# Second score pass on 128 rows for the dilated and grouped-query heads, with each key's two parts on both row halves

## The chip, the cores and the metric

The kernel runs on one core of one Trainium2 chip. The metric is device time in microseconds (us) of one launch; lower is better. A core has a matrix engine (TensorE, PE in the rows; its weight loads are PEld), a vector engine (VectorE, DVE), a scalar engine (ScalarE, ACT), a general engine (GpSimd, POOL) and an engine that issues the DMA transfers of this kernel (SyncE, SP). Each engine takes its own instructions in a fixed order.

## What is computed

The reference is an encoder of two layers on 512 tokens of width 1024. Each layer runs three groups of attention heads on the same input, projects their joined outputs and normalises, then runs a gated feed-forward block and normalises again. The part that the change touches is the first product of two of the three groups, in which every query meets every key:

```python
for l in range(DEPTH):                       # 2 layers
    h = x @ w_in[l]
    ...
    out_a = dense_attention(qa, ka, va, (64 + 32) ** -0.5)      # 6 latent heads, query and key of 96
    out_b = dilated_mixture(qb, kb, vb, rel_bias)               # 6 heads of 64, bias and mask per distance
    out_c = dense_attention(qc, kc, vc, 64 ** -0.5)             # 4 query heads on 2 key heads, of 64
    mix = concatenate([out_a, out_b, out_c]) @ w_out[l]
    x = layer_norm(ALPHA * x + mix)
    x = layer_norm(ALPHA * x + (silu(x @ w_gate[l]) * (x @ w_up[l])) @ w_down[l])
```

All data are 32-bit floats. The kernel keeps this accuracy by writing a number as a rounded first part plus a small second part and by multiplying the parts in separate passes, which add up in the same accumulator.

## The kernel before

The 512 tokens are four tiles of 128 rows. In each layer the work goes: value projection of the dilated heads, query and key projection of the first pair of dilated heads (`dil_qk(0)`), the attention proper (`attend`), the output projection, a normalisation, and the feed-forward block in two parts.

`attend` walks over 64 units, a unit being one head and one tile of 128 queries: six dilated heads, then four grouped-query heads, then six latent heads, four units each. For a unit, `Head.a` multiplies the query tile with all 512 keys into a bank `sc` (line 241), VectorE takes the minimum (line 247 for the dilated heads, which adds the bias tile `dt`; line 251 for the others), ScalarE the exponential (253), VectorE the reciprocal of the sum (255), and GpSimd the product into `pl` (256). One unit later `Head.b` transposes `pl` on TensorE into a bank `ptr` (264), and ScalarE and VectorE write its two parts `PTh` and `PTl` (271, 272). Another unit later `Head.c` multiplies with the values into `po` (282, 283). `sc` and `ptr` have two banks each, so a bank comes free only when VectorE has read it.

Between the units stand fillers: the projections of the next pairs (`dil_qk(1)`, `dil_qk(2)`, in the rows `qkp`), of the grouped-query heads (`g2`, rows `tp`), of the latent heads (`g1`, rows `tp`; `uq`, `uv`, `kT`), and part of the output projection (`opp`). A table `W` says at which units they begin and end. The tile framework's own scheduler then fixes the order of every engine's instructions from this program; so an edit at one place can move instructions elsewhere.

A head of 64 elements has a product of three passes: query first part with key first part, query second part with key first part, query first part with key second part. The query of a dilated or grouped-query head is stored with its two parts on the two halves of the 128 rows (`qa[:, e]`, first part on rows `64*e` and up). The key's first part lies on both halves, so one pass of all 128 rows does the first two products. The third is a second pass on the 64 rows of the query's first part:

```python
r, kc = cb(lst())
return [(qa[:, e, c], ka[:, kb]), (qa[r, e, c], kc)]
```

For a dilated pair the key comes from `dil_qk`: `dk` (a `pmix` slot) holds the two parts of both heads' keys, each head on its 64 rows, and `dqk` (a `pqk` slot) receives each head's first part on both halves by four copies on SyncE's queue (line 565). For the grouped-query heads both parts already lie on both halves (`gkk` holds each key head twice). The latent heads have queries and keys of 96 rows and three passes of 96 rows (`qk_of`).

One more place is spoken of below: the gains `gg` of the grouped-query heads are loaded at the start of each layer's program (line 410) into a single slot and scaled on VectorE (line 411). The scheduler puts the second layer's load and scaling into the first layer's attention, just behind the last use of the first layer's gains (line 430).

Of the kernel before, what the change touches and what calls it, by code (L numbers as in the profile page):

```python
# [10 lines left out]
F32 = mybir.dt.float32  # L11
# [5 lines left out]
P = 128  # L17
# [64 lines left out]
def encoder(ctx: ExitStack, tc, x, w_in, mla_q_norm, mla_kv_norm, w_uq, w_ukv, gqa_q_norm, gqa_k_norm, rel_bias,  # L82
# [59 lines left out]
    def wload(src, shape, lo, ring="w", raw="w"):  # L142
        # a weight chunk in two parts whose sum is exact
# [51 lines left out]
    def layer_norm(t, gb, end=False):  # L195
# [6 lines left out]
        if end:  # L202
            # nothing follows: the shortest way from the statistics to the result
# [16 lines left out]
    def load_gb(g, b):  # L220
        # the one-element copy holds the loads back until the slots are wanted
# [9 lines left out]
    class Head:  # L231
# [4 lines left out]
        def a(self, qt):  # L236
            # logits (negated), their minimum, exponentials over their sum
# [21 lines left out]
        def b(self, qt):  # L259
            # keys on partitions, in two parts  # L260
# [33 lines left out]
    class Pair:  # L294
        # the two heads of one 128-row tile of the mix
# [16 lines left out]
    def attend(heads, fillers):  # L312
        # the last pair goes by halves of the queries, so that the first half is done earlier
# [28 lines left out]
    def token_proj(xT, l, c0, c1, evac, lo, order=PAIRS, ws=None, pools=None):  # L342
        # order: (token tile, weight chunk) steps
# [24 lines left out]
    def bias_tables():  # L368
        # relative bias plus branch count, negated, as one vector over key - query
# [12 lines left out]
        # one copy a query, each a word further on, so that a row step of 1024 words shifts by one query  # L382
# [14 lines left out]
    for l in range(DEPTH):  # L397
        mix = [None] * 8

        # grouped-query heads: queries, keys, values with tokens on partitions  # L400
# [5 lines left out]
        # gains of the grouped-query heads, the query's with minus the logit scale  # L406
# [8 lines left out]
        def evac_g2(t, pb):  # L415
# [26 lines left out]
            # each query head in two parts side by side, each key head twice  # L442
# [10 lines left out]
        # dilated heads: values  # L453
# [7 lines left out]
        # latent projections  # L461
# [42 lines left out]
        def to_T(src, n, dst):  # L504
            # [tokens, n] tiles to [n, tokens] in two parts
# [35 lines left out]
        def dil_qk(pair):  # L541
            ws = [wload(krows(w_in[l], 0, KD, c + pair * P, c + pair * P + P), (P, KD, P), LO['qk'], QKR[pair]) for c in (C_Q, C_K)]
            yield
            for q, (h, o) in zip((True, False), ws):
# [5 lines left out]
                # per head: the query's two parts, the key's first part twice, on all partitions  # L550
                r = pqk.tile([P, 2, T], F32R, tag="q", name="dqk")
                if q:
                    sc = -(HD ** -0.5)
# [5 lines left out]
                else:  # L559
                    m = pmix.tile([P, 2, T], F32R, tag="m", name="dk")  # L560
                    A.copy(m[:, 0], pb)
                    V.tensor_tensor(m[:, 1], pb, m[:, 0].bitcast(F32), op=ALU.subtract)
                    for e in range(2):
                        for b in range(2):
                            nc.sync.dma_start(r[64 * b:64 * b + 64, e].bitcast(F32), m[64 * e:64 * e + 64, 0].bitcast(F32))
                    dqk[pair] += [r, m]
                yield

        def rope32(v, nh, tm):
            # v [P, NT, nh, 32], rotated in place  # L570
# [35 lines left out]
        def out_part():  # L606
            # the output projection of the pairs that are done, onto the residual
# [32 lines left out]
        def qk2_of(lst, e, kb, cb):  # L640
            # two passes: the query's two parts against the key's first, its first against the key's second
            def qk(qt):
                qa, ka = lst()[:2]
                c = slice(qt * P, (qt + 1) * P)
                r, kc = cb(lst())
                return [(qa[:, e, c], ka[:, kb]), (qa[r, e, c], kc)]
            return qk

        def qk_of(lst, e, n=64):
            # the three passes of one query tile; the stored order is (key, query) or (query, key) as told  # L650
# [8 lines left out]
        # told: what has been put into the program, for the asserts on the order of its parts  # L659
# [3 lines left out]
        for h in range(6):  # L663
            if h % 2 == 0:
                pr = Pair(mix, 3 + h // 2)
            heads.append(Head(qk2_of(lambda p=h // 2: dqk[p], h % 2, h % 2,
# [90 lines left out]
        for t in (2, 3):  # L757
            out_rest(t, (0, 1, 2))
            finish(t)
        xT = xT2[0]  # L760

        # feed-forward
        f0 = 0
        for part, nf in enumerate((12, 10)):
            act = []
# [96 lines left out]
```

## Time and profile before

| | |
|---|---|
| time, median of 3 runs | 1304.83 us (1304.62 to 1306.63) |
| span of the profiled execution, first to last instruction | 1300.4 us |
| outside the span, against the median | 4.4 us |
| TensorE busy | 1273.2 us, 98% |
| weight loads busy | 1057.4 us, 81% |
| VectorE busy | 678.0 us, 52% |
| ScalarE busy | 539.7 us, 42% |
| GpSimd busy | 323.4 us, 25% |
| first to last score of layer 1, of layer 2 | 60.6 to 269.6 us, 697.8 to 903.8 us |

How to read it: TensorE's busy time is a union of intervals whose ends are modelled, and one matmul's interval reaches into the next one's. So a busy TensorE may still be held up; what a matmul really takes is read from the distance between the starts of two matmuls that follow each other. The other engines' busy shares are means over stages of very different load.

### The profile page before, as it was taken

The page shows a single profiled execution, that of the slowest core. Times are in us where ns is not written, and L with a number is a line of the kernel's source. Part 1 is how long each engine was busy: PE and PEld are TensorE (multiplying, and loading weights), DVE is VectorE, ACT ScalarE, POOL GpSimd, SP SyncE. Part 2 cuts the span into 40 slices and gives each one's busy share as a digit, 9 for nine tenths or more (in the row PEclk, how much of TensorE's full clock was granted, in tenths as well). Part 3 has the DMA queues.
Part 4 walks back from the last instruction along what each step waited for, and adds up shares of the span by engine and source line. Part 5 has one row for each costly group of instructions (what it writes and reads, how often), then busy time and mean ns, then how long its engine had stood idle before and what let it go on. Part 6 is the DMA issues. An engine that isn't in the chain of part 4 may idle for free.

```text
span 1300.4 us, 16747 instructions
## 1 busy us (share of the span) xinstructions
PE 1273.2 (98%) x6352; PEld 1057.4 (81%) x6352; DVE 678.0 (52%) x1132; ACT 539.7 (42%) x949; POOL 323.4 (25%) x344
## 2 busy tenths in 40 slices
PE   8799899999999999999999999999999999999997
PEld 7678778879888888888897787888888888888885
DVE  4248788586333233333663778876933333333345
ACT  3256687554222212222244657866432221222222
POOL 0145465463000000000154455645700000000004
PEclk9899999999999999999999999999999999999999
DMA  6742310233333333332435222104343323333322
GB/s 189 205 120 76 96 33 18 89 99 97 101 96 97 97 97 97 98 98 97 148 87 148 59 88 70 38 13 130 87 118 97 96 93 94 101 96 96 97 101 109
DMA packets 142376, 125.72 MB, mean 97 GB/s; under 512 B 7212, under 2 KB 114860, under 8 KB 142296
## 3 DMA queue, kind: packets, MB, share of 16 engines
q1 hardware_dynamic: 142296, 124.66, 32.0%
q8 instruction: 50, 0.82, 0.3%
q14 instruction: 30, 0.25, 0.1%
HBM read 117.80 MB, written 5.27 MB: 95 GB/s over the span
## 4 chain that ended last, share of the span: by engine, by line
PE 89%; DMA 4%; DVE 4%; POOL 1%; ACT 1%; issue 0%; SPq 0%; DVEq 0%; POOLq 0%; ACTq 0%
PE up L167 6%; PE gate L167 6%; PE gate L165 6%; PE up L165 6%; PE gate L166 6%; PE up L166 6%; PE down L167 6%; PE sc L241 6%; PE down L165 6%; PE down L166 6%; PE ptr L264 4%; PE tp L166 2%; PE tp L167 2%; PE tp L165 2%; PE po L283 2%; PE po L282 2%
## 5 line engine op out<-in xcount | busy, mean ns | idle before, releaser
L152 ACT CAST whi<-wraw 128x1024 fp32r<-128x1024 f32 (+3 forms) x202 | 205.6, 1019 | 555.2 <-PE gate L166 146.3
L156 DVE TENSOR_TENSOR wlo<-wraw,whi 128x1024 fp32r<-128x1024 f32 (+3 forms) x170 | 208.3, 1227 | 319.6 <-ACT whi L152 315.4
L256 POOL TENSOR_TENSOR pl<-pl,srec 128x512 f32<-128x512 f32 x128 | 135.4, 1059 | 159.9 <-DVE srec L255 144.4
L191 POOL TENSOR_TENSOR rstd<-mv,eps_l 128x1 f32<-128x1 f32 x16 | 5.7, 358 | 680.6 <-DVE mv L200 680.6
L166 PE MATMUL gate<-xTl,whi 128*128 128x512 f32 (+1 forms) x384 | 142.8, 372 | 0.0
L166 PE MATMUL up<-xTl,whi 128*128 128x512 f32 (+1 forms) x384 | 142.7, 372 | 0.0
L167 PE MATMUL gate<-xTh,wlo 128*128 128x512 f32 (+1 forms) x384 | 142.7, 372 | 0.0
L167 PE MATMUL up<-xTh,wlo 128*128 128x512 f32 (+1 forms) x384 | 142.7, 372 | 0.0
L165 PE MATMUL up<-xTh,whi 128*128 128x512 f32 (+1 forms) x384 | 142.6, 372 | 0.0
L165 PE MATMUL gate<-xTh,whi 128*128 128x512 f32 (+1 forms) x384 | 142.4, 371 | 0.0
L167 PE MATMUL down<-whi,act 128*128 128x512 f32 x352 | 136.7, 389 | 0.0
L165 PE MATMUL down<-whi,act 128*128 128x512 f32 x352 | 136.7, 389 | 0.0
L166 PE MATMUL down<-wlo,act 128*128 128x512 f32 x352 | 136.7, 389 | 0.0
L156 POOL TENSOR_TENSOR wlo<-wraw,whi 128x512 fp32r<-128x512 f32 (+2 forms) x64 | 79.2, 1259 | 92.9 <-ACT whi L152 91.4
L776 DVE TENSOR_TENSOR sg<-sg,up 128x512 f32<-128x512 f32 x44 | 30.3, 688 | 135.8 <-PE up L167 134.4
L271 ACT CAST PTh<-ptr 128x512 fp32r<-128x512 f32 x128 | 74.9, 585 | 48.1 <-PE ptr L264 47.2
L272 DVE TENSOR_TENSOR PTl<-ptr,PTh 128x512 fp32r<-128x512 f32 x128 | 87.3, 683 | 13.5 <-ACT PTh L271 12.9
L166 PEld LDWEIGHTS up<-xTl,whi 128*128 128x128 f32 x384 | 72.3, 188 | 12.6
L167 PEld LDWEIGHTS up<-xTh,wlo 128*128 128x128 f32 x384 | 72.3, 188 | 12.4
L167 PEld LDWEIGHTS gate<-xTh,wlo 128*128 128x128 f32 x384 | 72.3, 188 | 12.5
L166 PEld LDWEIGHTS gate<-xTl,whi 128*128 128x128 f32 x384 | 72.3, 188 | 12.5
L165 PEld LDWEIGHTS gate<-xTh,whi 128*128 128x128 f32 x384 | 72.3, 188 | 12.4
(176 smaller groups left out, 2499.2 us busy)
## 6 DMA issues: line engine op xcount, KB each, us to landing
wraw<-in_ffn_w_down SPq DMA_DIRECT2D x54, 512.0 KB, 3.6
wraw<-in_ffn_w_up SPq DMA_DIRECT2D x44, 512.0 KB, 3.8
wraw<-in_ffn_w_gate SPq DMA_DIRECT2D x44, 512.0 KB, 3.8
wraw<-in_w_in SPq DMA_DIRECT2D x20, 512.0 KB, 4.2
wraw<-in_w_out SPq DMA_DIRECT2D x14, 512.0 KB, 3.7
dt<-skew SPq DMA_DIRECT2D x12, 448.0 KB, 3.1
wraw<-in_w_in SPq DMA_DIRECT2D x8, 416.0 KB, 3.3
wraw<-in_w_in SPq DMA_DIRECT2D x8, 384.0 KB, 3.8
```

The source lines that it names most:

```text
L152: A.copy(h[:, :n], r[:, :n])
L156: lo.tensor_tensor(o[:, c:c + step], r[:, c:c + step], h[:, c:c + step].bitcast(F32), op=ALU.subtract)
L165: TE.matmul(ps, ah, bh, start=first, stop=False)
L166: TE.matmul(ps, ah, bl, start=False, stop=False)
L167: TE.matmul(ps, al, bh, start=False, stop=last)
L241: TE.matmul(sc, a, b, start=i == 0, stop=i == len(ops) - 1)
L256: G.tensor_tensor(pl, pl, r.to_broadcast([P, T]), op=ALU.mult)
L264: TE.transpose(pb[:, kt * P:(kt + 1) * P], pl[:, kt * P:(kt + 1) * P], ident)
L271: A.copy(ph[:, :, c:c + P], pb)
L272: V.tensor_tensor(plo[:, :, c:c + P], pb, ph[:, :, c:c + P].bitcast(F32), op=ALU.subtract)
L282: TE.matmul(po[:, h0:h0 + 256], self.vst(kt), ph[:, kt], start=kt == 0, stop=False)
L776: V.tensor_tensor(sg, sg, pss[1], op=ALU.mult)
```

## The change

`qk2_of` now gives two passes of 128 rows with the same query operand: the key's first part on both halves, then the key's second part on both halves. The second pass so adds a fourth product, second part with second part, which was left out before. For that, each dilated head's key gets a tile `dk` of its own: its two parts are written on the head's own half by ScalarE and VectorE, and one copy of 64 rows and 1024 elements brings both to the other half. The first head of a pair takes its tile from `pqk`, the second from `pmix`, which are the slots that `dqk` and `dk` took. The grouped-query heads' data stay as they were. The file's comments are gone, and lines behind 639 stand one lower.

```diff
-                r = pqk.tile([P, 2, T], F32R, tag="q", name="dqk")
                 if q:
+                    r = pqk.tile([P, 2, T], F32R, tag="q", name="dqk")
                     sc = -(HD ** -0.5)
...
                 else:
-                    m = pmix.tile([P, 2, T], F32R, tag="m", name="dk")
-                    A.copy(m[:, 0], pb)
-                    V.tensor_tensor(m[:, 1], pb, m[:, 0].bitcast(F32), op=ALU.subtract)
                     for e in range(2):
-                        for b in range(2):
-                            nc.sync.dma_start(r[64 * b:64 * b + 64, e].bitcast(F32), m[64 * e:64 * e + 64, 0].bitcast(F32))
-                    dqk[pair] += [r, m]
+                        r = (pmix if e else pqk).tile([P, 2, T], F32R, tag="m" if e else "q", name="dk")
+                        a, b = slice(64 * e, 64 * e + 64), slice(64 - 64 * e, 128 - 64 * e)
+                        A.copy(r[a, 0], pb[a])
+                        V.tensor_tensor(r[a, 1], pb[a], r[a, 0].bitcast(F32), op=ALU.subtract)
+                        nc.sync.dma_start(r[b].bitcast(F32), r[a].bitcast(F32))
+                        dqk[pair].append(r)
...
-        def qk2_of(lst, e, kb, cb):
+        def qk2_of(lst, e):
             def qk(qt):
-                qa, ka = lst()[:2]
+                qa, ka = lst()
                 c = slice(qt * P, (qt + 1) * P)
-                r, kc = cb(lst())
-                return [(qa[:, e, c], ka[:, kb]), (qa[r, e, c], kc)]
+                return [(qa[:, e, c], ka[:, 0]), (qa[:, e, c], ka[:, 1])]
             return qk
...
-            heads.append(Head(qk2_of(lambda p=h // 2: dqk[p], h % 2, h % 2,
-                                     lambda q, r=slice(64 * (h % 2), 64 * (h % 2) + 64): (r, q[2][r, 1])), lambda kt, h=h: dv[kt][:, h], h % 2, pr.mf,
+            heads.append(Head(qk2_of(lambda p=h // 2, e=h % 2: (dqk[p][0], dqk[p][1 + e]), h % 2),
+                              lambda kt, h=h: dv[kt][:, h], h % 2, pr.mf,
...
-                heads.append(Head(qk2_of(lambda kv=kv: gqk[kv][::-1], e, 0, lambda q: (slice(0, 64), q[1][0:64, 1])), lambda kt, kv=kv: gv[kt][:, kv], e, pr.mf,
+                heads.append(Head(qk2_of(lambda kv=kv: gqk[kv][::-1], e), lambda kt, kv=kv: gv[kt][:, kv], e, pr.mf,
```

The scheduler's order moves with it, in the part of the program between the first unit and the latent heads alone. TensorE at the first scores of layer 1, before (the numbers tell buffers apart: `sc_447` and `sc_486` are the first two units' score banks, `dqk_393` the query, `dqk_423` and `dk_424` the key):

```order
L241 MATMUL sc_447<-dqk_423,dqk_393 128x512
L241 MATMUL sc_447<-dk_424,dqk_393 128x512
L241 MATMUL sc_486<-dqk_423,dqk_393 128x512
L241 MATMUL sc_486<-dk_424,dqk_393 128x512
L165 MATMUL tp_571<-whi_460,xTh_124 128x512
L166 MATMUL tp_571<-wlo_462,xTh_124 128x512
```

The same place of the changed program, where x2 are the two passes of one unit:

```order
L241 MATMUL sc_447<-dk_423,dqk_393 128x512 x2
L241 MATMUL sc_486<-dk_423,dqk_393 128x512 x2
L165 MATMUL tp_571<-whi_460,xTh_124 128x512
L166 MATMUL tp_571<-wlo_462,xTh_124 128x512
L167 MATMUL tp_571<-whi_460,xTl_125 128x512
```

The place is the same, and both passes of a unit now read one key tile.

SyncE's queue behind the first two weight chunks of the grouped-query projection in layer 1, before:

```order
L150 DMA wraw<-in_w_in 128x2x512 x2
L565 DMA dqk<-dk 64x512 x4
L150 DMA wraw<-in_w_in 128x2x512
L565 DMA dqk<-dk 64x512 x2
L150 DMA wraw<-in_w_in 128x2x512
L565 DMA dqk<-dk 64x512 x2
L150 DMA wraw<-in_w_in 128x8x128
```

And in the changed program:

```order
L150 DMA wraw<-in_w_in 128x2x512 x2
L565 DMA dk<-dk 64x1024 x2
L150 DMA wraw<-in_w_in 128x2x512 x2
L565 DMA dk<-dk 64x1024 x2
L150 DMA wraw<-in_w_in 128x8x128
```

Four copies of the first pair became two at the same place, and those of the second pair now stand behind two weight chunks instead of behind one and two.

VectorE around the scaling of the second layer's gains, in the first layer's attention, before (`g2_1130` is the last token tile of the grouped-query projection; `sc_1166` and `sc_1224` are scores of units 15 and 16):

```order
L429 TENSOR_TENSOR g2_1130<-g2_1130,rstd_1139 128x384
L446 TENSOR_TENSOR g2_1094<-rt_1108,g2_1094 128x4x64
L430 TENSOR_TENSOR g2_1130<-g2_1130,gg_215 128x384
L247 ISA pl_1169,nm_1170<-sc_1166,dt_831 128x512
L247 ISA nm_1170 128x1
L290 TENSOR_TENSOR mf_1196<-po_1033,pvt_1194 64x512
L439 TENSOR_TENSOR g2_1130<-g2_1130,tab_114 128x384
L255 RECIPROCAL srec_1174<-ssum_1172 128x1
L441 TENSOR_TENSOR rt_1144<-g2_1130,rt_1144 128x384
L247 ISA pl_1227,nm_1228<-sc_1224,dt_1068 128x512
L247 ISA nm_1228 128x1
L446 TENSOR_TENSOR g2_1130<-rt_1144,g2_1130 128x4x64
```

behind which `L411 TENSOR_SCALAR gg_5785<-gg_5785` and the reciprocal of `sc_1224`'s unit follow. In the changed program:

```order
L430 TENSOR_TENSOR g2_1130<-g2_1130,gg_215 128x384
L272 TENSOR_TENSOR PTl_1302<-ptr_1296,PTh_1301 128x4x128
L247 ISA pl_1169,nm_1170<-sc_1166,dt_831 128x512
L247 ISA nm_1170 128x1
L290 TENSOR_TENSOR mf_1196<-po_1033,pvt_1194 64x512
L439 TENSOR_TENSOR g2_1130<-g2_1130,tab_114 128x384
L255 RECIPROCAL srec_1174<-ssum_1172 128x1
L441 TENSOR_TENSOR rt_1144<-g2_1130,rt_1144 128x384
L247 ISA pl_1227,nm_1228<-sc_1224,dt_1068 128x512
L247 ISA nm_1228 128x1
L446 TENSOR_TENSOR g2_1130<-rt_1144,g2_1130 128x4x64
L411 TENSOR_SCALAR gg_5785<-gg_5785 128x256
```

One subtraction (`PTl_1302<-ptr_1296`), which stood behind line 411, now stands ahead of it; the scaling itself, and the reciprocal behind it, stay where they were.

## Rows read from the trace of the kernel before

**Rows 1.** The page's part 1: busy us (share of the span) xinstructions.
```profile
PE 1273.2 (98%) x6352; PEld 1057.4 (81%) x6352; DVE 678.0 (52%) x1132; ACT 539.7 (42%) x949; POOL 323.4 (25%) x344
```
**Rows 2.** Timeline, TensorE and its weight loads, one unit's scores: start us, us, then the instruction.
```profile
102.45 0.40 PE L241 MATMUL sc<-dqk 128*128 128x512 f32 x1
102.78 0.18 PEld L241 LDWEIGHTS sc<-dk,dqk 64*128 64x128 f32 x1 [0.25 <-issue]
102.78 0.50 PE L241 MATMUL sc<-dk,dqk 64*128 64x512 f32 x1
103.21 0.19 PEld L283 LDWEIGHTS po<-PTl,dv 128*128 128x128 f32 x1 [0.25 <-issue]
103.21 0.39 PE L283 MATMUL po<-PTl,dv 128*128 128x256 f32 x1
```
**Rows 3.** Timeline, TensorE and its weight loads, passes of 128 rows in the feed-forward block.
```profile
400.11 0.39 PE L166 MATMUL gate<-xTl,whi 128*128 128x512 f32 x1
400.34 0.39 PE L167 MATMUL gate<-xTh,wlo 128*128 128x512 f32 x1
...
400.12 0.19 PEld L167 LDWEIGHTS gate<-xTh,wlo 128*128 128x128 f32 x1
```
**Rows 4.** Line 241 (scores): count, duration ns min/median/max, first and last start, forms.
```profile
L241 PE MATMUL sc<-qkT,gqT x64: 387/492/502, 158.7 to 830.8; 128*128 128x512 f32 x32, 64*128 64x512 f32 x32
...
L241 PE MATMUL sc<-dk,dqk x48: 491/498/792, 61.3 to 789.9; 64*128 64x512 f32 x48
```
**Rows 5.** Timeline, TensorE, one unit's scores of a latent head (three passes of 96 rows).
```profile
238.85 0.86 PE L241 MATMUL sc<-kT,qkT 96*128 96x512 f32 x3
239.55 0.60 PE L264 MATMUL ptr<-tab,pl 128*128 128x128 f32 x4
```
**Rows 6.** Waits of TensorE in the two attention stages: us in total, times, longest us.
```profile
PE sc L241 <- DMA dqk<-dk: 7.0, 1, 7.0
PE po L283 <- DVE PTl L272: 1.8, 2, 1.4
...
PE po L283 <- DVE PTl L272: 0.7, 2, 0.4
```
**Rows 7.** Timeline, VectorE and TensorE around the second layer's gains, in layer 1.
```profile
127.34 0.55 DVE L430 TENSOR_TENSOR g<-g,gg 128x384 f32<-128x384 f32 x1
137.86 0.29 DVE L411 TENSOR_SCALAR gg<-gg 128x256 f32<-128x256 f32 x1 [5.89 <-DMA gg<-in_gqa_q_norm]
139.54 0.68 DVE L272 TENSOR_TENSOR PTl<-ptr,PTh 128x512 fp32r<-128x512 f32 x1
...
140.37 0.63 PE L264 MATMUL ptr<-tab,pl 128*128 128x128 f32 x4 [1.66 <-POOL rstd L192]
```
**Rows 8.** Stretches: us, then PE, PEld, DVE, ACT, POOL busy (instructions), clock, DMA.
```profile
137.80:166.00 28.20, 24.68 (x144) 19.30 (x143) 26.18 (x69) 21.35 (x52) 16.34 (x20) 1.00 0.33 99
783.00:800.00 17.00, 16.16 (x99) 12.27 (x98) 15.49 (x37) 13.76 (x35) 10.02 (x12) 1.00 0.27 87
187.00:220.00 33.00, 33.00 (x206) 27.80 (x207) 30.91 (x62) 28.49 (x65) 20.84 (x20) 1.00 0.08 21
```
**Rows 9.** Stretches, the scores of line 241 alone: us, PE (passes), PEld.
```profile
127.30:166.00 38.70, 9.40 (x22) 4.08 (x22) 1.00 0.30 89
783.00:800.00 17.00, 5.28 (x12) 2.23 (x12) 1.00 0.27 87
188.00:197.00 9.00, 3.25 (x8) 1.49 (x8) 1.00 0.10 30
```
**Rows 10.** The key tile `dk` and its copies; then, layer 2's first subtraction and first score.
```profile
L562 DVE TENSOR_TENSOR dk<-qkp,dk x6: 684/688/692, 43.4 to 759.0; 128x512 fp32r<-128x512 f32 x6
...
DMA to landing us min/median/max: 2.2/3.1/11.1
...
692.66 0.69 DVE L562 TENSOR_TENSOR dk<-qkp,dk 128x512 fp32r<-128x512 f32 x1 [3.91 <-ACT dk L561]
...
697.75 0.39 PE L241 MATMUL sc<-dqk 128*128 128x512 f32 x1
```

## The prediction

> **What bounds the kernel now.** The page's first part comes first: TensorE is busy 98% of the span and no other engine over 52%, weight loads apart [rows 1]. That alone does not say that TensorE is at its pace, because the intervals of matmuls overlap. So the second view is the timeline, read by starts. In the feed-forward block a pass of 128 rows and 512 columns follows the one before after 0.23 us (400.11 to 400.34), and the next weight load (0.19 us) lies under the running pass [rows 3]: nothing can be gained there but by fewer passes. At a score of a dilated head it looks different [rows 2]: the first pass, on 128 rows, holds TensorE from 102.45 to 102.78, which is 0.33 us, and the second, on 64 rows, from 102.78 to 103.21, which is 0.43 us. The reader is to see that the weight load of the 64-row pass does not lie under the pass before it. It starts with its own pass, after 0.25 us in which the load path had no reason to wait that the profile shows, and the same happens once more at the 128-row pass behind. So a unit's two passes take 0.76 us, where two plain ones take 0.46.
>
> The third view is the waits. In the two attention stages TensorE waits little: 7.0 us once for the first key copies of layer 1, 1.8 us and 0.7 us for VectorE's `PTl` [rows 6], and 1.66 us more for one transpose [rows 7]. The last views are VectorE's timeline and the stretches, because VectorE is the engine that TensorE would meet next: it is busy 26.18 of 28.20 us at 137.8 to 166, 15.49 of 17 at 783 to 800, and 30.91 of 33 at 187 to 220 [rows 8].
>
> **The change, part by part.**
>
> *The second pass on 128 rows.* It removes the two pauses of a unit. What a second full pass costs instead is bounded by 0.23 us, as every plain pass of 128 rows [rows 3], and by the 0.43 us of the pass that it replaces. I take 0.23, because the nearest rows are those of the latent heads: their scores are written to the same banks by the same line, three passes on 96 rows, and the three take 0.70 us (238.85 to 239.55), 0.23 each [rows 5]. They have fewer than 128 rows too and show no pause, so the pause belongs to the 64-row form. One unit saves 0.76 - 0.46 = 0.30 us. There are 48 units of dilated and 32 of grouped-query heads in the two layers [rows 4], so 80 x 0.30 = 24.0 us. At the upper bound of the price nearly nothing is saved but the first pause, 80 x 0.10 = 8 us.
>
> *The key tiles.* Each of six pairs gets one more cast and one more subtraction; I take the subtraction's 0.69 us of today [rows 10] for each of the two, since both have 512 columns. Six more on VectorE are 4.1 us, covered by TensorE's projection passes that stand between a pair's keys and its first score. If none of it were covered, it would cost those 4.1 us.
>
> *The copies.* Four of 128 KB become two of 256 KB. The first score needs the same bytes as before, at the same place of SyncE's queue, but its copy now also waits for the subtraction. In layer 1 TensorE waits for it already; the cost there is 0 to 0.69 us, and I take 0, because the wait is 7.0 us [rows 6] and the slowest copy landed 11.1 us after its issue [rows 10], which is queueing behind other transfers and not work on the key. In layer 2 the subtraction ends at 693.35; with the median landing of 3.1 us the copy is there at 696.5, and the first score starts at 697.75 [rows 10]. That cover is 1.3 us; gone, it would cost what the copy is later. On SyncE's queue the second pair's copies now stand behind one more weight chunk, with four units of the first pair's second head still to run ahead of their first use; cost nothing.
>
> *Where VectorE gives it back.* A saving on TensorE counts only where VectorE keeps up. I go through the three stretches in which it hardly idles.
>
> First, layer 1 from 127.3 to 166. The second layer's gains are loaded when line 430 has read the first layer's, and VectorE then stands 5.89 us at line 411 [rows 7]. From 127.34 to 137.86 the length is set by that load, and from there to 166 VectorE is busy 26.18 of 28.20 us [rows 8]. TensorE waits in this stretch now, and if it comes sooner it waits longer. The stretch holds 22 of the passes, 11 units [rows 9]: 11 x 0.30 = 3.3 us held back, of a possible 0 to 3.3. The order moves one subtraction of 0.68 us (at 139.54 [rows 7]) ahead of line 411, into the time in which VectorE stands; the third pair's extra key subtraction, 0.69 us, stands ahead of line 430. The two cancel.
>
> Second, layer 2 from 783 to 800, without a gains load but with the same work: 12 passes, 6 units [rows 9], 1.8 us. Without them the stretch would be 15.2 us, and VectorE has 15.49 us of work in it [rows 8]. So I take all 1.8 back, of 0 to 1.8.
>
> Third, the end of the grouped-query heads and the first latent units, 187 to 220 in layer 1, and its counterpart in layer 2. Four units lie in it (8 passes [rows 9]), 1.2 us; without them 31.8 us would remain for 30.91 us of VectorE's work [rows 8], 97%. That fits just, so I take half, 0.6 us in each layer, 1.2 in all, of 0 to 2.4.
>
> *Sum.* 24.0 - 3.3 - 1.8 - 1.2 = 17.7 us. The profiled execution's span is 1300.4 us; the median of the runs lies 4.4 us above it, which I leave as it is. 1300.4 - 17.7 + 4.4 = 1287.1 us.
>
> **The rivals.**
>
> *All of it comes through.* VectorE's backlogs shift with TensorE instead of holding it, because TensorE also feeds VectorE. For it: in each layer VectorE has slack outside the three stretches, and 97% is no refusal. Against it: line 411's wait does not depend on TensorE's pace. Time: 1304.8 - 24.0 = 1280.8 us.
>
> *VectorE becomes the bound through the whole dense part*, from the third pair to the last grouped-query unit, 24 units in each layer. For it: the three shares above, all over 90%. Against it: TensorE's waits for VectorE are 0.7 us in all of layer 2's attention today [rows 6]. It would hold back 48 x 0.30 = 14.4 us, leave 9.6, and give 1295.2 us.
>
> *The pause stays.* It could belong to the second pass as such, or to the tile that it reads. Against it: the latent heads' second and third passes [rows 5]. Then the time is today's, 1304.8 us.
>
> *Slower: the weight loads stand bare.* A 128-row load cannot run under a 128-row pass into the same rows, so every score pass pays its 0.19 us in the open: 2 x (0.23 + 0.19) = 0.84 us for a unit where it is 0.76 now, 80 x 0.08 = 6.4 us more, 1311 us. It decides from 0.15 us a load on, when the two loads of a unit eat up the 0.30. Against it: the load at 400.12 lies under the pass at 400.11, both of 128 rows [rows 3].
> The Trainium skill has this rule: "TensorE: Matmul & The Clock Gate", in Part 3 under what overlaps and what doesn't, says that weight loads overlap running matmuls only when their row group differs. By that rule the change takes away the only loads that could overlap. The trace disagrees with it: the loads that do not overlap are those at the change of the row count.
>
> **How the numbers follow.** The forecast gets 0.56: its mechanism on TensorE is shown by rows, and its three deductions are each bounded. All of it 0.25; VectorE the bound throughout 0.15; the pause stays 0.03; slower 0.01. The forecast's own range, with its deductions between a third and one and a half times their size, is 1283 to 1290. For 8 in 10 the range takes in the case of no deduction and about half of the case in which VectorE bounds all: 1279.8 to 1293.5 us. A difference under 0.2%, 2.6 us, cannot be told from no change here. All cases but the last two are faster by more: faster 0.96, same 0.03, slower 0.01.
>
> **What would show it right or wrong.** In the profile after, line 241 should have only forms of 128 and 96 rows, with starts 0.23 us apart and weight loads under the pass before. If a unit still takes 0.76 us, the first step is wrong. VectorE's wait at line 411 should still be near 5.9 us, and TensorE's waits for `PTl`, for the transposes and for `pl` between 125 and 165 should grow by some 3 us, those of layer 2 between 775 and 800 by some 2. If they don't, the first rival holds. If waits of that kind appear throughout from 165 to 200 and 800 to 835, the second does. The wait for the first copy should stay near 7 us, and none should appear at layer 2's first score. What would make the prediction wrong most easily is the scheduler's new order: rows moved in the fillers can place a transpose or a value pass closer behind the work that it waits for than any row here can show.

## The result

| | before | changed |
|---|---|---|
| median of the timed runs | 1305.36 us (4 runs, 1304.62 to 1306.63) | 1290.45 us (4 runs, 1289.81 to 1292.91) |
| ratio, 95% interval | | 0.9889 (0.9875 to 0.9903) |
| span of the profiled execution | 1300.4 us | 1288.0 us |

The kernel became 14.5 us faster by the ratio (12.7 to 16.3), 14.9 by the medians; 17.7 were forecast. The page of the changed kernel, part 1, beside [rows 1]:

```profile
PE 1252.6 (97%) x6352; PEld 1065.2 (83%) x6352; DVE 688.0 (53%) x1138; ACT 543.1 (42%) x955; POOL 323.2 (25%) x344
```

The instruction count of TensorE is the same, so the same passes take less time. Line 241 of the changed kernel by forms, as in [rows 4]:

```profile
L241 PE MATMUL sc<-kT,qkT x144: 389/395/482, 193.5 to 891.6; 96*128 96x512 f32 x144
...
L241 PE MATMUL sc<-dk,dqk x96: 388/396/764, 61.5 to 777.3; 128*128 128x512 f32 x96
...
L241 PE MATMUL sc<-qkT,gqT x64: 387/397/775, 157.4 to 816.3; 128*128 128x512 f32 x64
```

The 64-row form is gone. One unit's scores on the timeline of the changed kernel, to be set beside [rows 2] (x2 is two passes in one row):

```profile
110.32 0.39 PE L167 MATMUL qkp<-xTh,wlo 128*128 128x512 f32 x1
110.32 0.41 PEld L241 LDWEIGHTS sc<-dk,dqk 128*128 128x128 f32 x2
110.55 0.62 PE L241 MATMUL sc<-dk,dqk 128*128 128x512 f32 x2
...
111.01 0.60 PE L264 MATMUL ptr<-tab,pl 128*128 128x128 f32 x4
```

From 110.55 to 111.01 the two passes take 0.46 us, where they took 0.76, and their weight loads lie under the passes before. So the gain on TensorE is the forecast one, and the question is where the rest of 80 x 0.30 = 24.0 us went. The waits of TensorE in the changed kernel, first at 125 to 165 us, then at 775 to 800 us (us in total, times, longest):

```profile
PE po L283 <- DVE PTl L272: 2.7, 2, 2.3
PE ptr L264 <- POOL pl L256: 1.9, 2, 1.6
PE sc L241 <- DVE nm L247: 0.9, 1, 0.9
PE po L282 <- ACT PTh L271: 0.6, 1, 0.6
PE ptr L264 <- DVE g L481: 0.2, 1, 0.2
...
PE po L283 <- DVE PTl L272: 2.3, 1, 2.3
PE po L282 <- ACT PTh L271: 0.6, 1, 0.6
PE ptr L264 <- POOL pl L256: 0.3, 1, 0.3
```

In each layer there is now one wait of 2.3 us for `PTl`, behind the scores of unit 23, the last dilated one, where it was 1.4 and 0.4 [rows 6]. And a second loss stands beside the waits. Stretches of the changed kernel (us, then PE, PEld, DVE, ACT, POOL busy, the granted clock, DMA):

```profile
134.00:137.00 3.00, 1.28 (x7) 0.94 (x8) 2.60 (x10) 1.07 (x5) 2.52 (x5) 1.00 0.01 3
137.00:141.00 4.00, 4.00 (x14) 3.64 (x14) 3.27 (x9) 3.45 (x8) 2.09 (x3) 0.57 0.00 0
...
150.00:154.00 4.00, 1.45 (x7) 0.59 (x4) 3.96 (x9) 3.43 (x10) 3.69 (x5) 1.00 0.14 18
154.00:158.00 4.00, 3.65 (x16) 3.57 (x17) 3.10 (x9) 1.40 (x3) 0.58 (x1) 0.57 0.32 115
...
778.00:782.00 4.00, 1.44 (x10) 1.24 (x11) 3.97 (x9) 2.34 (x8) 2.86 (x4) 1.00 0.42 130
782.00:786.00 4.00, 4.00 (x20) 3.66 (x19) 4.00 (x11) 2.21 (x5) 1.04 (x1) 0.57 0.14 40
```

Three times TensorE stands for most of 3 to 4 us, and the 4 us behind are granted 0.57 of full speed: some 3.4 us at half clock (1.2 in place of 2.4 GHz), and (1 - 0.57) x 4 = 1.7 us lost each time, 5.1 in all. Before, the clock is 1.00 in these stretches [rows 8]. At one place the change has less of it: behind the wait for layer 1's first key both kernels run at half clock, before with 0.50 at 62 to 66 us and 0.91 at 66 to 70, changed with 0.56 and 1.00.

To place gains and losses, the attention stages are cut at the starts of scores. Layer 2 of the changed kernel, first pass of unit 0, 16, 28 and 40 (the first latent one):

```profile
693.63 0.39 PE L241 MATMUL sc<-dk,dqk 128*128 128x512 f32 x1
...
757.32 0.39 PE L241 MATMUL sc<-dk,dqk 128*128 128x512 f32 x1
...
793.89 0.39 PE L241 MATMUL sc<-qkT,gqT 128*128 128x512 f32 x1
...
819.53 0.40 PE L241 MATMUL sc<-kT,qkT 96*128 96x512 f32 x1
```

The distances of these starts, layer 1 / layer 2, in us, and for the latent heads up to the last score, in all kernels of this study (one profiled execution each; the ratio to the kernel before is from timed runs):

| kernel | ratio (95% interval) | units 0 to 16 | 16 to 28 | 28 to 40 | latent |
|---|---|---|---|---|---|
| before | 1 | 68.9 / 68.8 | 40.7 / 37.8 | 28.9 / 28.9 | 71.0 / 70.9 |
| changed | 0.9889 (0.9875 to 0.9903) | 64.4 / 63.7 | 42.0 / 36.6 | 25.7 / 25.6 | 71.4 / 72.1 |
| 1 key tiles alone | 1.0033 (1.0021 to 1.0045) | 70.7 / 69.3 | 42.9 / 39.2 | 28.9 / 28.9 | 71.3 / 71.6 |
| 2 grouped-query alone | 0.9952 (0.9938 to 0.9965) | 69.7 / 68.8 | 41.3 / 37.4 | 25.6 / 25.7 | 71.4 / 72.2 |
| 3 dilated alone | 0.9935 (0.9923 to 0.9947) | 64.3 / 63.7 | 44.0 / 38.0 | 28.9 / 28.9 | 71.1 / 71.3 |
| 4 weights held | 0.9901 (0.9888 to 0.9914) | 64.4 / 63.7 | 41.6 / 35.8 | 24.4 / 24.4 | 75.1 / 75.6 |
| 5 rotation on GpSimd | 0.9869 (0.9854 to 0.9884) | 64.4 / 63.8 | 40.6 / 35.3 | 25.9 / 25.9 | 72.5 / 72.5 |
| 6 relief | 0.9863 (0.9850 to 0.9877) | 64.3 / 63.7 | 40.7 / 35.2 | 25.9 / 25.9 | 72.5 / 72.5 |
| 7 relief, kernel before | 0.9974 (0.9963 to 0.9985) | 69.5 / 68.7 | 39.4 / 36.6 | 28.9 / 28.9 | 71.1 / 71.0 |
| 8 two gain buffers | 0.9911 (0.9898 to 0.9925) | 64.0 / 63.7 | 38.3 / 37.6 | 25.6 / 25.6 | 71.4 / 71.4 |
| 9 key tiles, relief | 1.0009 (1.0000 to 1.0018) | 69.9 / 69.3 | 40.0 / 37.6 | 28.4 / 28.4 | 72.5 / 72.5 |
| 10 scratch tile | 0.9882 (0.9868 to 0.9895) | 63.1 / 61.7 | 42.1 / 37.7 | 25.3 / 25.3 | 72.5 / 72.5 |
| 11 four units ahead | 0.9983 (0.9972 to 0.9993) | 63.8 / 62.9 | 44.8 / 40.4 | 26.8 / 26.7 | 72.4 / 72.0 |
| 12 relief, no gains wait | 0.9829 (0.9816 to 0.9843) | 64.4 / 63.7 | 35.5 / 35.1 | 25.9 / 25.9 | 72.5 / 72.5 |

In units 0 to 16 4.5 and 5.1 us come through, of 2 x 16 x 0.30 = 9.6. In units 16 to 28 layer 1 loses 1.3 and layer 2 gains 1.3, of 3.6 each. In 28 to 40 6.5 of 7.2 us are left, and the latent heads, which the change doesn't touch, lose 0.4 and 1.2. The sum is 14.4 us for both layers. The two spans differ by 12.4 us only: 0.9 are lost ahead of layer 1's first score, and 1.1 between the two attention stages.

These distances hold more than the passes. The half clock behind the first key's wait is shorter in the changed kernel, and some 1.0 of the 4.5 us comes from that. And the scheduler's order moves other work across the cuts: in the changed kernel units 0 to 16 of each layer hold 60 transposes (line 264) and 52 value passes (lines 282 and 283), where they held 56 and 48, and one projection pass more; units 16 to 28 hold as many fewer. At 0.11, 0.14 and 0.20 us each, their means in units 16 to 28 of layer 2 before, that is about 1.2 us a layer (an estimate). In layer 2 three projection passes, 0.7 us, left units 0 to 16 for a place ahead of the first score. So a stretch can be compared cleanly only between kernels in which TensorE's order is the same. By the traces it is the same, instruction for instruction, in the changed kernel and runs 1 and 3, in the kernel before and run 2, and in runs 6, 9 and 12.

### The profile page after: what moved, and what is told of

It reads as the page before. It is cut to its first block, busy times and chain, and to the rows that moved or that the text cites. A ratio compares the mean times of both kernels' runs of the same rounds, so it can differ in the third digit from the quotient of the medians.

```text
span 1288.0 us, 16749 instructions
## 1 busy us (share of the span) xinstructions
PE 1252.6 (97%) x6352; PEld 1065.2 (83%) x6352; DVE 688.0 (53%) x1138; ACT 543.1 (42%) x955; POOL 323.2 (25%) x344
## 4 chain that ended last, share of the span: by engine, by line
PE 84%; DVE 6%; DMA 4%; ACT 3%; POOL 2%; issue 1%; DVEq 0%; SPq 0%; POOLq 0%; ACTq 0%
PE down L167 6%; PE gate L165 6%; PE down L165 6%; PE up L167 6%; PE up L165 6%; PE down L166 6%; PE gate L167 6%; PE up L166 6%; PE gate L166 6%; PE sc L241 4%; PE ptr L264 3%; PE tp L165 2%; PE tp L166 2%; PE tp L167 2%; PE po L283 2%; PE po L282 2%
## 5 line engine op out<-in xcount | busy, mean ns | idle before, releaser
L271 ACT CAST PTh<-ptr 128x512 fp32r<-128x512 f32 x128 | 75.0, 586 | 38.0 <-PE ptr L264 37.4
L167 PEld LDWEIGHTS gate<-xTh,wlo 128*128 128x128 f32 x384 | 72.4, 189 | 12.5
L166 PEld LDWEIGHTS up<-xTl,whi 128*128 128x128 f32 x384 | 72.4, 189 | 12.5
L165 PEld LDWEIGHTS up<-xTh,whi 128*128 128x128 f32 x384 | 72.4, 188 | 12.5
L167 PEld LDWEIGHTS up<-xTh,wlo 128*128 128x128 f32 x384 | 72.3, 188 | 12.4
```

The lines of the kernel that those rows point to most:

```text
L165: TE.matmul(ps, ah, bh, start=first, stop=False)
L166: TE.matmul(ps, ah, bl, start=False, stop=False)
L167: TE.matmul(ps, al, bh, start=False, stop=last)
L271: A.copy(ph[:, :, c:c + P], pb)
```

## The experiments

Theory at first: VectorE falls behind in units 16 to 28 because TensorE comes sooner, and the stalls bring the half clock. Rivals: each unit saves less than 0.30 us; the new key tiles cost something.

**1. The key tiles alone.** The changed kernel, second pass back on 64 rows (`r` are the rows of the query's first part).

```diff
-return [(qa[:, e, c], ka[:, 0]), (qa[:, e, c], ka[:, 1])]
+return [(qa[:, e, c], ka[:, 0]), (qa[r, e, c], ka[r, 1])]
```

> Only the new key tiles (one more cast and subtraction a pair, two copies of 256 KB); the second pass stays on 64 rows in all heads. If the key tiles and their copies cost nothing, as predicted: within 2 us of the kernel before (1305 us). Rival, that the missing gain went into the key tiles (six subtractions, later copies): slower than before by 4 to 10 us.

Slower by 0.0033 x 1306.7 = 4.3 us (2.7 to 5.9): the rival holds. The run prices the tiles together with the order that the scheduler makes for them: 340 of TensorE's 6352 instructions stand at another place than before. The wait for `PTl` and the half clock are there without any faster pass. Its TensorE waits at 125 to 170 and 775 to 810 us, and three stretches:

```profile
PE po L283 <- DVE PTl L272: 2.1, 1, 2.1
...
PE sc L241 <- DVE nm L247: 0.9, 1, 0.9
...
PE ptr L264 <- POOL pl L256: 0.6, 1, 0.6
...
PE po L283 <- DVE PTl L272: 2.1, 1, 2.1
```

```profile
145.00:149.00 4.00, 4.00 (x12) 3.17 (x12) 3.26 (x9) 3.12 (x8) 2.08 (x2) 0.57 0.00 0
162.00:166.00 4.00, 3.80 (x16) 3.32 (x16) 3.24 (x9) 1.40 (x3) 0.71 (x2) 0.57 0.30 107
800.00:804.00 4.00, 3.99 (x17) 3.12 (x18) 3.63 (x10) 1.40 (x3) 1.10 (x2) 0.58 0.26 95
```

So 3.6 of the changed kernel's 6.3 us of waits in layer 1, 2.1 of its 3.2 in layer 2, and as much half clock, are in a kernel whose passes are the old ones. (The profiled execution is the slowest of this run's six, 1312.79 us at a mean granted clock of 0.989; the others have 0.991.)

**2. Grouped-query heads alone.** The kernel before, one argument changed.

```diff
-lambda q: (slice(0, 64), q[1][0:64, 1])
+lambda q: (slice(0, 128), q[1][:, 1])
```

> Second pass on 128 rows in the 32 grouped-query units alone, dilated heads as before. If a unit saves 0.30 us and what was given back lies ahead of these units (near the last dilated ones): 8 to 9.6 us faster than before, 1296 to 1297 us. Rival, that every unit saves only its share of the gain, 0.18 us: 6 us faster, 1299 us.

6.3 us faster (4.6 to 8.1), of 32 x 0.30 = 9.6. The size is the rival's, but not for its reason: units 28 to 40 give 6.5 of 7.2 us, 0.27 a unit. What is missing lies in the crowded stretch before them, in the latent heads, and in the first 16 units of layer 1, which the edit doesn't touch: they take 0.8 us more, at a clock of 0.56 from 66 to 70 us where it was 0.91 before.

**3. Dilated heads alone.** The changed kernel, with the grouped-query heads' second pass on rows 0 to 63.

> New key tiles and second pass on 128 rows in the 48 dilated units alone; grouped-query heads stay on 64 rows. If a unit saves 0.30 us, 14.4 us gross, and the new stalls of 1 to 2.6 us at the units 16 to 24 of each layer stand against it: 5 to 8 us faster than before, 1297 to 1300 us, with TensorE's wait of some 2.5 us for PTl still there in both layers. Rival, 0.18 us a unit: 9 us faster. Rival, all of it comes through in the dilated heads: 14 us faster.

8.5 us faster (6.9 to 10.1): a little more than the theory's 5 to 8, and nearer to the 9 of the rival with 0.18 us a unit. The place refutes that rival: units 0 to 16 win 4.6 and 5.1 us, 0.30 a unit, and the wait of 2.3 us for `PTl` is there in both layers. Against run 1, which has the same key tiles, it is 0.9935 / 1.0033 = 0.9902, 12.8 us of 14.4. So runs 1 to 3 add up: +4.3 for the key tiles, -12.8 for the dilated passes, -6.3 for the grouped-query ones, together -14.8 where the change has -14.5.

**4. Weights held back.** Why is `PTl` late? VectorE and then GpSimd of the changed kernel just before the 2.3 us wait of layer 2 ends at 780.95:

```profile
776.80 1.05 DVE L474 TENSOR_SCALAR g<-g,rstd 128x256 f32<-128x256 f32 x1
777.77 1.28 DVE L475 TENSOR_SCALAR g<-g,rstd 128x128 f32<-128x128 f32 x1
778.98 0.15 DVE L255 RECIPROCAL srec<-ssum 128x1 f32<-128x1 f32 x1
779.05 0.15 DVE L478 TENSOR_TENSOR krt<-g,tab 128x16 f32<-128x16 f32 x1
779.12 0.16 DVE L479 TENSOR_TENSOR krt<-g,tab 128x16 f32<-128x16 f32 x1
779.32 0.97 DVE L480 TENSOR_TENSOR g<-g,tab 128x32 f32<-128x32 f32 x1
780.21 0.68 DVE L272 TENSOR_TENSOR PTl<-ptr,PTh 128x512 fp32r<-128x512 f32 x1
```

```profile
776.42 2.56 POOL L156 TENSOR_TENSOR wlo<-wraw,whi 128x512 fp32r<-128x512 f32 x2
779.21 1.04 POOL L256 TENSOR_TENSOR pl<-pl,srec 128x512 f32<-128x512 f32 x1 [0.23 <-DVE srec L255]
```

Three small operations take about 1 us each. Line 475 ends at 779.05, as GpSimd's `wlo` does (778.98), and line 480 at 780.29, as GpSimd's `pl` does (780.25). So this run holds back the output projection's first weights, whose `wlo` that is, until the first grouped-query pair is done.

```diff
-        r = raws[raw][0].tile([P, 1024], F32, tag=raws[raw][1], name="wraw")
+        r = raws[raw][0].tile([P, 1024], F32, tag=raws[raw][1], name="wraw"); hold is not None and V.tensor_copy(r[0:1, 0:1], hold[0:1, 0, 0:1].bitcast(F32))
...
-                    w = wload(krows(w_out[l], k0, n, half * 512, half * 512 + 512), (P, n, 512), LO['opp'])
+                    w = wload(krows(w_out[l], k0, n, half * 512, half * 512 + 512), (P, n, 512), LO['opp'], hold=None if half else mix[6])
```

> The changed kernel, with the first output-projection weights held back until the first grouped-query pair is done, so that GpSimd no longer subtracts them while VectorE works off the latent projection. Theory: VectorE's small operations at lines 474 to 480 stand until GpSimd's instruction beside them ends; without it they take 0.15 to 0.35 us again, TensorE's 2.6 us wait for PTl falls under 0.8 us in both layers, and the kernel is 3 to 4 us faster than the changed one, 1286 to 1288 us. Rival, that PTl is late because of the order of VectorE's and ScalarE's instructions alone: the wait stays at 2 us or more, and the time within 1 us of 1290.

VectorE of this run at the same work:

```profile
780.92 0.18 DVE L478 TENSOR_TENSOR krt<-g,tab 128x16 f32<-128x16 f32 x1
781.01 0.35 DVE L474 TENSOR_SCALAR g<-g,rstd 128x256 f32<-128x256 f32 x1
781.28 1.06 DVE L475 TENSOR_SCALAR g<-g,rstd 128x128 f32<-128x128 f32 x1
...
782.95 0.18 DVE L480 TENSOR_TENSOR g<-g,tab 128x32 f32<-128x32 f32 x1
```

Line 474 is back at 0.35 us and line 480 at 0.18. Line 475 meets another GpSimd instruction, `pl` from 781.08 to 782.25, and takes 1.06. TensorE's wait for `PTl` falls from 2.3 to 1.4 us in both layers, less far than expected. Units 16 to 28 of layer 2 become 0.7 us shorter. But the time isn't better than the changed kernel's: the held weights come due in the latent heads, which lose 3.7 and 3.5 us. The cause of the slow operations is shown; the gain was put at the wrong place.

**5. The rotation on GpSimd** (lines 478 to 481, `V.tensor_tensor` to `G.tensor_tensor`).

> The changed kernel, with the four small operations of the key's rotation (lines 478 to 481) on GpSimd in place of VectorE. Theory: on VectorE they stand behind GpSimd's instruction that runs at the time (line 480 took 0.9 us where it takes 0.2 alone); on GpSimd itself they can't meet one. TensorE's 2.6 us wait for PTl in both layers falls under 1 us and the kernel is 2 to 4 us faster than the changed one. Rival, that GpSimd becomes late with pl instead: within 1 us of the changed one, with TensorE waiting for GpSimd's pl.

**6. Relief:** the scalings on ScalarE besides.

```diff
+G.tensor_scalar(gm[:, i, 0:2], gm[:, i, 0:2], -MLA_SCALE, None, op0=ALU.mult)
...
-V.tensor_scalar(g[:, :256], g[:, :256], r[:, 0:1], -MLA_SCALE, op0=ALU.mult, op1=ALU.mult)
-V.tensor_scalar(g[:, 256:384], g[:, 256:384], r[:, 1:2], None, op0=ALU.mult)
+A.activation(g[:, :256], g[:, :256], AF.Copy, scale=r[:, 0:1])
+A.activation(g[:, 256:384], g[:, 256:384], AF.Copy, scale=r[:, 1:2])
```

> As the run before, and the two scalings of the latent projection (lines 474 and 475) on ScalarE too, their constant folded into the gains once. VectorE has no operation of the latent projection's evacuation left. Theory: the 2.6 us wait goes in both layers, 3 to 6 us faster than the changed kernel, 1284 to 1287 us. Rival, that ScalarE is the late one there: the wait for PTl becomes one for PTh, within 1 us of the changed one.

Run 5 is 2.6 us below the changed kernel by the difference of the ratios, give or take 2.7, so not clear of none; run 6 3.4, give or take 2.5. The long wait for `PTl` is gone in both (0.7 us at most is left), and in layer 2 the clock stays at 1.00. In layer 1 TensorE still waits up to 2.2 and 1.9 us at once for GpSimd's `pl`. Stretches of run 6:

```profile
125.00:170.00 45.00, 39.12 (x236) 34.11 (x235) 28.49 (x66) 34.01 (x87) 25.20 (x43) 0.96 0.26 77
765.00:800.00 35.00, 32.60 (x219) 28.24 (x218) 26.80 (x57) 30.32 (x74) 21.59 (x29) 1.00 0.26 80
```

**7. The same relief in the kernel before.**

> The same relief put into the kernel before (second pass on 64 rows, old key tiles). Theory: there these operations met GpSimd less, and TensorE waited only 1.7 and 0.7 us, so it gains 1 to 2.5 us, less than the changed kernel does by the same edit; the distance between the two relieved kernels is then 17 to 21 us, where it is 14.5 without. Rival, that the relief is worth the same in both: the distance stays at 14 to 15 us.

It gains 3.4 us as well (2.0 to 4.8). The distance between the two relieved kernels is 0.9974 - 0.9863 = 0.0111, 14.5 us, give or take 2.3, the same as without. So the rival holds: VectorE's slowed operations cost some 3 us in either kernel, and within that interval they are not what this change lost.

**8. Two buffers for the gains** (`pgg` from 1 to 2).

> The changed kernel with two buffers for the gains, so that the second layer's are loaded without waiting for line 430 of the first. Theory: VectorE's 4.6 us at line 411 go, TensorE's waits of 1.8 and 1.0 us at 134 to 137 with them, and the half clock behind them: 2 to 4 us faster than the changed kernel, in layer 1 alone. Rival, that VectorE's place in line 411 is free time: within 1 us of the changed one.

Neither: 2.9 us slower than the changed kernel by the ratios, give or take 2.5. Layer 1's units 16 to 28 take 38.3 us in place of 42.0, as the theory has it. But the scheduler put the second layer's line 411 at the program's start, where VectorE waited 8.4 us for both gains. TensorE waited 4.5 us there for VectorE's `xTl`, and the first score came at 67.3 us, 5.8 later. A wait was moved, not taken away.

**9. Key tiles with the relief.**

> The run with the new key tiles alone (second pass on 64 rows), with the relief of lines 474 to 481 put in, to be set beside the kernel before with the same relief (1303 us, ratio 0.9974). Theory: the key tiles cost 4 us because they shift VectorE's small operations onto GpSimd's long ones; without these they cost nothing, ratio 0.996 to 0.999. Rival, that the two extra instructions a pair cost it by themselves: still 4 us more, ratio 1.000 to 1.002.

1.0009 beside run 7's 0.9974: 0.0035, 4.6 us (2.7 to 6.4). Stretches of this run:

```profile
130.00:170.00 40.00, 37.58 (x208) 29.00 (x207) 25.11 (x59) 28.85 (x75) 22.56 (x42) 1.00 0.28 86
...
770.00:800.00 30.00, 29.31 (x162) 23.10 (x161) 18.47 (x43) 24.18 (x63) 18.88 (x36) 1.00 0.32 96
```

No stretch of units 16 to 28 is at half clock in this run, and yet the key tiles cost in sum what they cost in run 1. The sum that the rival named holds; that the extra instructions make it by themselves is not shown, since TensorE's order differs between the two runs as well. By the table the cost also lies elsewhere. Against run 7, units 0 to 16 take 1.0 us more in both layers together, units 16 to 28 1.6, units 28 to 40 1.0 less, and the latent heads 2.9 more, in part because seven value passes a layer that stood ahead of the first latent score now stand behind it. Beside run 6, which has the same order of TensorE, the faster passes are worth 1.0009 - 0.9863 = 0.0146, 19.1 us, give or take 2.1.

**10. A scratch tile**, one cast and one subtraction of 128 rows a pair.

```diff
+if e == 0: m = pmix.tile([P, 2, T], F32R, tag="m", name="dkm")
+if e == 0: A.copy(m[:, 0], pb)
+if e == 0: V.tensor_tensor(m[:, 1], pb, m[:, 0].bitcast(F32), op=ALU.subtract)
...
-A.copy(r[a, 0], pb[a])
-V.tensor_tensor(r[a, 1], pb[a], r[a, 0].bitcast(F32), op=ALU.subtract)
-nc.sync.dma_start(r[b].bitcast(F32), r[a].bitcast(F32))
+for b in range(2): nc.sync.dma_start(r[64 * b:64 * b + 64].bitcast(F32), m[64 * e:64 * e + 64].bitcast(F32))
```

> The changed kernel with one cast and one subtraction of 128 rows a pair into a scratch tile, as in the kernel before, and four copies of 256 KB out of it in place of two. If the extra instructions a pair on ScalarE and VectorE are what the key tiles cost: 3 to 4 us faster than the changed kernel, ratio 0.986 to 0.987. Rival, that the copies are late: TensorE's first wait in layer 1 grows from 7.0 us and the time is that of the changed kernel or more, ratio 0.989 or above.

The time of the changed kernel. Units 0 to 16 are 1.3 and 2.0 us shorter, but they hold 13 and 12 TensorE instructions fewer; units 16 to 28, with 15 more, take 1.2 us more in layer 2, and the first score comes 2.8 us later (64.3 us). Fewer instructions, more copies and another order weigh the same here, so this run doesn't tell which part of the key tiles costs the time.

**11. Scores four units ahead** (`LA` from 3 to 4, `ppl` from 4 to 5 tiles, and the layer norm's statistics in a pool of their own).

> The changed kernel with the scores four units ahead of their transposes in place of three (five tiles for the exponentials; the layer norm's statistics in three small tiles to make room). Theory, that what is held back is a matter of time between the steps of a unit and not of VectorE's work in sum: most of TensorE's waits in the dense stretches go and it is 4 to 8 us faster than the changed kernel, ratio 0.983 to 0.986. Rival, that VectorE's work in sum sets the pace there: within 2 us of the changed kernel, ratio 0.987 to 0.990.

12 us slower than the changed kernel, outside both expectations. Units 16 to 28 take 2.8 and 3.8 us more, units 28 to 40 1.1 in each layer. Part of the first is 15 more TensorE instructions in that stretch, but the waits that the theory wanted gone grew too: 7.8 and 4.3 us in units 16 to 28, where the changed kernel has 6.3 and 3.2. So more lead does not help in the dense stretch. The rest of the loss lies behind the attention stages; why it hurts was not followed up.

**12. Relief without the gains' wait.** The scale is taken out of line 411 and put on where the query is split.

```diff
-V.tensor_scalar(gg[:, 0:4], gg[:, 0:4], -(HD ** -0.5), None, op0=ALU.mult)
...
-A.copy(gq[:, :, 0].bitcast(F32R), tq4)
-V.tensor_tensor(gq[:, :, 1], tq4, gq[:, :, 0], op=ALU.subtract)
+A.activation(gq[:, :, 0].bitcast(F32R), tq4, AF.Copy, scale=-(HD ** -0.5))
+V.scalar_tensor_tensor(gq[:, :, 1], tq4, -(HD ** -0.5), gq[:, :, 0], op0=ALU.mult, op1=ALU.subtract)
```

> The relief of lines 474 to 481, and the scaling of the query gains (line 411) taken out: the logit scale is put on where the query's two parts are made, so VectorE has nothing left to wait for in the gains' load. Theory: in layer 1 that wait is what TensorE's waits at 134 to 146 us and the half clock behind them come from; they go, layer 1 comes down to the waits of layer 2, and the kernel is 3 to 5 us faster than with the relief alone (ratio 0.9863), 0.982 to 0.984. Rival, that VectorE has no time to win in layer 1, since its work behind the wait is as long as TensorE's: within 1.5 us of the relief alone, ratio 0.985 to 0.9875.

As the theory has it: 0.9829, 4.4 us under run 6, give or take 2.5, median 1283.78 us, the fastest of all. Stretches of this run:

```profile
125.00:170.00 45.00, 42.56 (x273) 37.37 (x272) 33.02 (x74) 37.76 (x96) 29.73 (x48) 1.00 0.26 77
765.00:800.00 35.00, 32.61 (x221) 27.96 (x220) 27.43 (x58) 31.79 (x77) 23.18 (x32) 1.00 0.25 74
```

Layer 1's units 16 to 28 fall from 40.7 to 35.5 us, next to layer 2's 35.1, and the clock stays at 1.00. In run 6 the gains' load cost layer 1 some 5 us there, of which 1.7 was half clock.

## Why the prediction was right, and where not

**The second pass: right.** 0.46 us a unit as forecast. In units 0 to 16 of layer 2, where the clock is full and TensorE waits for nothing, the 32 score passes, each taken from its start to the next instruction's, hold TensorE for 7.45 us where it was 12.25: 4.8 of 4.8 us. That the two stretches together win 9.6 of 9.6 is partly luck, since some 1.0 us of it is clock, and some 1.7 us of moved work stands against it. The rival of bare weight loads is refuted by the row at 110.32. By the Trainium skill's rule that this rival stood on ("TensorE: Matmul & The Clock Gate", Part 3) loads of the same rows would not overlap; here they do.

**The key tiles, "covered by TensorE's projection passes": this is the step that failed.** They were costed at nothing and cost 4.3 us alone (2.7 to 5.9). That is near the 4.1 us that the prediction named for the case of no cover, but it did not arise as it was put there, as six subtractions laid bare one behind the other: in run 1 units 0 to 16 grow by 1.8 and 0.6 us, which is about what the moved work and a longer half clock behind the first key's wait (0.50 still at 66 to 70 us) make; units 16 to 28 grow by 2.2 and 1.3 although that work has left them, with TensorE's waits in layer 2 up from 0.7 to 2.1 us and three stretches at half clock, 5.1 us. Run 9 removes the half clock, and a cost of the same size stands in other places. Which of the extra instructions, the copies and the scheduler's new order makes it is open.

**Where VectorE gives it back: right in sum.** Taken on top of the key tiles, the faster passes bring 0.9889 / 1.0033 = 0.9857, 18.7 us, give or take 2.4. 17.7 were forecast. So of 24.0 us 5.3 are held back, where 3.3 + 1.8 + 1.2 = 6.3 were deducted. By place, with the key tiles in: units 16 to 28 hold back 4.9 us in layer 1 and 2.3 in layer 2, the later units and latent heads 0.7 + 1.6. From run 1 to the changed kernel, in the same order of TensorE, it is 2.7, 1.0 and 1.3, near the forecast 3.3, 1.8 and 1.2; by these two profiles units 0 to 16 win 2.3 us more than 9.6, 1.8 of it clock. That VectorE's work in sum sets the pace there, as the deductions supposed, is not shown: the long waits are each for one late operation, and the relief that takes the longest away is worth as much in the kernel before.

**The gains' load in layer 1: right in mechanism.** VectorE's lines 430 and 411 in the changed kernel, beside [rows 7]:

```profile
123.99 0.56 DVE L430 TENSOR_TENSOR g<-g,gg 128x384 f32<-128x384 f32 x1
...
133.31 0.29 DVE L411 TENSOR_SCALAR gg<-gg 128x256 f32<-128x256 f32 x1 [4.60 <-DMA gg<-in_gqa_q_norm]
```

The wait is 4.6 us where "near 5.9" was said, and TensorE's waits at 125 to 165 us grew from 3.5 to 6.3 us, those at 775 to 800 from 0.7 to 3.2, where "some 3" and "some 2" were forecast. In layer 2 that is partly luck: run 1, without a faster pass, already waits 2.1 us there, so the passes add 1.1 and the key tiles 1.4. In layer 1 run 1 waits 3.6 us, and the passes add 2.7. Run 12 shows that this load holds layer 1 back, with the relief in: TensorE's order is run 6's, and units 16 to 28 fall by 5.2 us in layer 1 and by 0.1 in layer 2.

**The copies: right, with some luck.** The first wait for `dk` was 6.9 us, and layer 2's first score waited for none. But its copy took 4.0 us to land, not 3.1: issued at 688.7, it was there 0.9 us ahead of the score at 693.63, and 0.7 of that are three projection passes that the new order puts ahead of the score.

**Not foreseen: the half clock.** The prediction counted a stall once. Three of the new stalls have 3.4 us at half speed behind them, 1.7 us lost each time, while the forecast knew a stall only by its own length. They come with the key tiles: run 1 has three of the same length. The shorter half clock behind the first key's wait gives some 1.0 us back. How much of the 5.1 us reaches the end is not measured by itself, since the relief that takes two of the three away (run 6) takes other waits away too.

**Open.** With the relief in and no half clock, layer 2's units 16 to 28 win 2.4 of 3.6 us from run 9 to run 6 (37.6 to 35.2), in the same order of TensorE. The missing 1.2 us are waits: TensorE's sum there grows from 1.1 to 2.3 us. They are each under 1 us and for three different engines, so no single one of them was found to be the bound.

## What to carry to other kernels

A pause that shows between two starts on the busiest engine can be counted, and it comes back one for one where the other engines have room; cut the stage at fixed units to see where it doesn't, and compare the cuts only between kernels that have the same order. Measure the preparation that a faster pass needs by itself, with the old pass: here it cost 4.3 us against 18.7 won, though the work had looked covered. In a stretch where TensorE already waits, count a new stall twice, once as a wait and once for the clock that may fall behind it, and look first for a load that a helper engine waits for: here that was worth 4.4 us.

## What the hardware showed that was not expected

- A VectorE operation on data in SBUF stood until the 128 x 512 instruction that GpSimd had begun before it ended: line 480, 128 x 32 elements, 0.97 us at 779.32 and 0.18 in run 4 at 782.95; line 474 1.05 and 0.35. In run 4 line 480 ran beside a GpSimd operation of 128 x 2 elements (782.81 to 783.51) and wasn't held. `PTl`, which reads one operand from PSUM, took 0.67 to 0.69 us throughout the changed kernel. The Trainium skill has it: "SBUF — State Buffer", under who interferes with whom, says that a VectorE instruction with two inputs in SBUF, or one in a mode that uses both ports, which `tensor_scalar` can enter, contends with GpSimd for a shared port pair, and that whoever issues second is blocked for the whole of the other's instruction. The trace agrees for the 128 x 512 instructions; the 128 x 2 one does not show it.
- After it had been busy for only 1.28 of 3 us (134 to 137), 1.45 of 4 (150 to 154) and 1.44 of 4 (778 to 782), TensorE ran some 3.4 us at half clock, though it was nearly always busy then. The kernel before, with waits of 1.66 us at 140 [rows 7] and 1.4 us [rows 6], kept 1.00 there [rows 8].
